# Beginning one layer's modulation vectors a stage earlier, with a result moved to another buffer

## The chip, the cores and the metric

The kernel runs on one core of a Trainium2 chip. The metric is the device time of one execution in microseconds (us), as the median of several runs. A core has five engines that work side by side, each through its own queue in order: TensorE (PE; its weight loads are PEld), VectorE (DVE), ScalarE (ACT), GpSimd (POOL) and SyncE (SP), which here issues nearly all the loads from memory. TensorE's clock has two levels, 1.2 and 2.4 GHz; the profile gives the granted clock as a share of the higher one.

## What the kernel computes

Two blocks are chained over 256 tokens of width 1024. Block 1 has 16 more tokens in front (272 in all) and two layers; block 2 has two layers, each with a vector of six modulation parts made from `c`. Cut to what matters here:

```python
# block 1, layer 0 ("ab"): attention and a convolution, then the output products
a = sliding_window_sink_attention(q, k, v, sinks) * silu(g_a)
c = silu(layer_norm(causal_depthwise_conv(u, conv_w, conv_b), ln_g, ln_b))
c = (c @ w_pw2) * silu(g_b)
y = concatenate([a, c], axis=-1) @ w_out
h = h + rms_norm(y, ab_post_norm)
# block 1, layer 1 ("sb")
y = (stick_breaking_attention(q, k, v) * silu(g)) @ w_out      # q, k, v, g = h' @ w_in
h = h + rms_norm(y, sb_post_norm)
# block 2, layer l: the modulation vectors, and what they are needed for
mod = (silu(c) @ ada_w[l] + ada_b[l]).reshape(6, D)            # ada_w[l]: 1024 x 6144
sh1, sc1, g1, sh2, sc2, g2 = mod
h = rmsnorm(x, norm_mix[l]) * (1 + sc1) + sh1                   # layer 0 ("ev"): mixer, then
x = x + g1 * mixer(h)
h = rmsnorm(x, norm_ffn[l]) * (1 + sc2) + sh2
x = x + g2 * peer(h, ...)                                       # a mixture of 16384 experts
```

`mod` depends on `c` alone, so it can be computed at any time before the "ev" layer uses it.

## The kernel before

**The main work.** Each product of a layer is cut into units of 512 KB of weights. `take` hands the next unit to the product, `load` fetches units some steps ahead into the ring `raw` (slots raw_70 and raw_71, two units each), and `prep` splits a unit into `hi` (ACT, L159) and `lo` (POOL, L261, partly DVE, L263), since most products are taken as three passes. The products of the "ab" layer use the weights as they come (kind "n"), so nothing is prepared for them, and DVE, ACT and POOL have little to do while its output products run. The order of all instructions is that in which the program is written; no scheduler moves them.

**Background work.** `after_unit` is called behind each unit. It emits the work that belongs to finished results (`pend`, `follow`, `hooks`) and then calls `tick(ns)`, which draws from two lanes of generators, `bgs` and `bg1`, as many steps as fit into `ns` (for bgs) and `ns1` (for bg1) nanoseconds of a nominal cost. What it draws is written into the engines' queues at that place.

**The modulation vectors** are such generators (`ada`, made by `ada_pool` into `ada0`). One step works on half a load, 128 x 512 numbers. In lane bgs a step is one DVE instruction (L677 or L679) at a nominal 660 ns, and after four loads the sum is transposed and reduced (L687, L688). In lane bg1 a step is a scaling on ACT and an addition on POOL (L675) at a nominal 1300 ns. The 40 loads (L654, 512 KB each, 32 for bgs and 8 for bg1) are issued on SP into the tile `scratch`, three buffers for bgs and two for bg1, each as soon as its buffer has been read; SP's queue waits there. The rest of the vectors (of layer 1, and the last two parts of layer 0) are made later, in the mixture.

**Where they run before.** `_build` puts ada0 into the lanes just ahead of `sb_layer`; its products tick 1400 ns a unit. What is left is drawn in the output products of "sb" and in the "ev" layer.

**The "ab" layer's end.** `linear_o(2, ...)` computes the output products in two halves (e = 0, 1) of four units. `need(0)`, at its start, waits out attention and convolution and drains the lanes; `need(2)` runs the layer norm and the product with `w_pw2` in between. `post_in` squares the results (ACT), adds the squares (DVE, L749, tile `absq`) and writes the scaled results to `y`: the first four by ACT, the last four by DVE (L757). `rest` then sums over partitions on PE, makes the reciprocal root (ACT, then DVE L485, L486, L488), and `add_post` scales, adds and writes the input `h` of the "sb" layer (DVE L772, POOL L778, ACT, DVE L527). `scratch` held the attention's scores and weights until then, and before the change it also holds `y`.

In the "sb" layer DVE scales the first products by the norm `sbr` (L1167), in the "ev" layer by the norm `r` (L1376, L1378); only then their PSUM banks are free for the next products (there are four banks with the tag "mm").

Of the kernel before, what the change touches and what calls it, by code (L numbers as in the profile page):

```python
# [43 lines left out]
KC = D // P  # L44
# [73 lines left out]
class _Kernel:  # L118
# [665 lines left out]
    def ab_layer(self, pool):  # L784
        nc, a, T = self.nc, self.a, T1
# [16 lines left out]
        ch = tl([P, KC, T], "cat")  # L802
        zh = tl([P, 4, T], "z")
        sc = self.scratch
# [245 lines left out]
        def layer_norm(rest):  # L1050

            sq = pool.tile([P, 4, T], F32, name="lnsq", tag="sq0")
            rl = pool.tile([P, T], F32, name="lnr")

            def total(x):
                ps = self.bank("aux")
                for c in range(4):
                    nc.tensor.matmul(ps[:, :T], self.ones, x[:, c, :], start=(c == 0), stop=(c == 3))
                return ps

            def mean():
                nc.gpsimd.tensor_add(cv[:, 2, :], cv[:, 2, :], part[:, 0, :])
                nc.gpsimd.tensor_add(cv[:, 3, :], cv[:, 3, :], part[:, 1, :])
                nc.vector.tensor_add(part[:, 2, :], part[:, 2, :], part[:, 3, :])
                nc.vector.tensor_add(cv[:, 3, :], cv[:, 3, :], part[:, 2, :])
                ps = total(cv)
                for c in range(4):
                    nc.vector.scalar_tensor_tensor(out=cv[:, c, :], in0=ps[:, :T], scalar=-1.0 / 512,
                                                   in1=cv[:, c, :], op0=ALU.mult, op1=ALU.add)
                    self.act(sq[:, c, :], cv[:, c, :], "Square")  # L1070

            def var():
                ps = total(sq)
                self.rsqrt(rl, ps[:, :T], 512, 1, pool, "")
                for c in range(4):
                    nc.vector.tensor_mul(cv[:, c, :], cv[:, c, :], rl)
                for c in range(4):
                    self.act(zh[:, c, :], cv[:, c, :], "Silu", scale=self.v["conv_ln_g"][:, c:c + 1],
                             bias=self.v["conv_ln_b"][:, c:c + 1])
                self.act(gb, gb, "Silu")  # L1080
            return [mean, var]
# [4 lines left out]
        def need(j):  # L1086
            if j == 0:
                while self.steps or self.follow or self.pend:
                    self.after_unit(800.0)
                self.drain()  # L1090
                self.hooks += layer_norm(None)
            if j == 2:
                self.flush()
                self.mark('ab_pw2')
                self.linear(2, (zh, None), T, c_out, kc=4, tags=("aux", "s"))
                self.flush()
# [2 lines left out]
        self.linear(11, (self.hn, None), T, consume, ns=2500, late=1)  # L1099
        self.pool_share = 0.5  # L1100
        self.mark('ab_out')
        y = sc[:, :KC * T].rearrange("p (c t) -> p c t", c=KC)
        sq = pool.tile([P, T], F32, name="absq", tag="vT")
        post = self.post_in(y, sq, self.v["ab_post_norm"], T, pool)
        self.linear_o(2, (ch, None), T, post, need=need)
        self.mark('ab_post')
        r2 = post.rest()
        nxt = self.scale(self.xT, self.v["sb_pre_norm"])
# [1073 lines left out]
def _build(ctx, tc, aps, const, out, stage=99, dbg=None):  # L2182
    ctx.enter_context(tc.manual_schedule())
    k = _Kernel(ctx, tc, aps, const)
    k.v_done = 0
    k.chain = stage == 99

    def phase(name):
        st = ExitStack()
        return st, st.enter_context(tc.tile_pool(name=name, bufs=1))  # L2190

    specs = []
    if stage in (1, 2, 99):
        specs += k.ab_specs() + k.sb_specs()
    if stage in (3, 4, 99):
        specs += k.ev_specs()
    if stage in (4, 99):
        specs += k.peer_specs(0)
    if stage in (5, 99):
        specs += k.od_specs()  # L2200
    if stage == 99:
        specs += k.peer_specs(1)
    k.plan(specs)
    k.mark('setup')
    pa = ExitStack()
    k.scratch = pa.enter_context(tc.tile_pool(name="ada", bufs=1)).tile([P, 7296], F32, name="scratch")
    ada0 = k.ada_pool(0, stage != 99)
    b1 = ExitStack()
    p1 = b1.enter_context(tc.tile_pool(name="block1", bufs=1))
    k.xT = p1.tile([P, KC, T1], F32, name="xT")  # L2210
    if stage in (1, 2, 99):
        st, pool = phase("ab")
        k.hn = pool.tile([P, KC, T1], F32, name="hn")
    k.setup()
    if stage in (1, 2, 99):
        k.ab_layer(pool)
        st.close()
        if stage > 1:
            with ExitStack() as st:
                pool = st.enter_context(tc.tile_pool(name="sb", bufs=1))  # L2220
                if stage == 99:
                    k.bgs += ada0[0]
                    k.bg1 += ada0[1]
                k.sb_layer(pool)
    if stage in (3, 4, 5):
        tc.nc.vector.tensor_copy(k.x2, k.xT[:, :, NM:])
    if stage != 1:
        b1.close()
    if stage in (3, 4, 99):
        k.mark('ev')  # L2230
        st, pool = phase("ev")
        if stage != 99:
            k.use_ps("aux")
            for g in ada0[0] + ada0[1]:
                for _ in g:
                    pass
        if not k.chain:
            nxt = k.enter(0, 0)
            for c in range(KC):
                nxt(c)  # L2240
        k.ev_layer(pool)
        st.close()
    pa.close()
    if stage in (4, 99):
        k.peer(0, k.ada_slots(1) if stage == 99 else None)
    if stage in (5, 99):
        k.mark('od')
        st, pool = phase("od")
        if stage == 5:
            k.use_ps("aux")  # L2250
            for g in sum(k.ada_pool(1), []):
                for _ in g:
                    pass
            for _ in k.angles(pool.tile([P, 770], F32, name="ang")):
                pass
        if not k.chain:
            nxt = k.enter(1, 0)
            for c in range(KC):
                nxt(c)
        k.od_layer(pool)  # L2260
        st.close()
    if stage == 99:
        k.peer(1, None, out)
    if dbg is not None:
        tc.nc.sync.dma_start(dbg[:, :, NM:], k.x2)
        tc.nc.sync.dma_start(dbg[:, :, :NM], k.x2[:, :, :NM])
# [21 lines left out]
```

## Time and profile before

| | |
|---|---|
| median of 3 runs | 2330.15 us (2322.14 to 2331.12) |
| profiled execution, its own time | 2316.25 us |
| its span, first to last instruction | 2314.5 us |
| busy: PE, PEld | 95%, 85% |
| busy: DVE, ACT, POOL | 76%, 56%, 75% |
| mean granted clock of TensorE | 0.984 |
| output products of "ab" | 127 to 175 us |
| "sb" layer | 180 to 367 us |
| "ev" layer | 374 to 462 us |

The profiled execution took 1.75 us more than its span, and 13.9 us less than the median of the runs. The modulation vectors of the lanes run from 193 us (first load) to 405 us (last reduction); the mixtures, which take most of the time, come after 462 us.

### The profile page before, as it was taken

What the parts mean: (1) busy time and instruction counts of PE and PEld (TensorE: products, weight loads), DVE (VectorE), ACT (ScalarE), POOL (GpSimd) and SP (SyncE); (2) the same over time, 40 slices, a digit from 0 to 9 for tenths busy, and PEclk for the clock granted to TensorE, in tenths of its full rate; (3) what the DMA queues carried; (4) which work ended last, traced back from release to release, by engine and by line L of the source; (5) the groups of instructions that cost most, each with busy time, mean ns of one, the idle gap of its engine ahead of it and who ended that gap; (6) DMA issues with size and microseconds to landing.
All of it is one profiled execution on the core that took longest, in us unless ns stands there. A gap on an engine that the chain in (4) does not pass through costs nothing. (4 is left out here: it accounts for less than half of the span.)

```text
span 2314.5 us, 42145 instructions
## 1 busy us (share of the span) xinstructions
PE 2194.9 (95%) x14789; PEld 1972.2 (85%) x14789; DVE 1763.1 (76%) x3502; ACT 1292.1 (56%) x2608; POOL 1735.9 (75%) x2070
## 2 busy tenths in 40 slices
PE   8997997899989999999999988998899999999997
PEld 6776987898989999888787877998889999888886
DVE  5927888578787999668989776786869998565555
ACT  2424575464436888544444645554458886545444
POOL 1106878788999988877576685579899888777776
PEclk9999998999999999999999999999999999999999
DMA  5326655378878778568888533687777876555554
GB/s 164 110 79 217 236 177 188 124 197 163 164 153 167 159 153 161 167 247 292 314 287 300 185 103 103 191 168 149 160 160 161 159 154 158 192 199 182 200 186 141
DMA packets 285582, 414.88 MB, mean 179 GB/s; under 512 B 16489, under 2 KB 217386, under 8 KB 285370
## 3 DMA queue, kind: packets, MB, share of 16 engines
q1 hardware_dynamic: 279722, 405.30, 63.7%
q10 hardware_dynamic: 5648, 6.89, 1.1%
q8 instruction: 116, 1.90, 0.4%
q14 instruction: 96, 0.79, 0.1%
HBM read 408.98 MB, written 3.15 MB: 178 GB/s over the span
## 5 line engine op out<-in xcount | busy, mean ns | idle before, releaser
L261 POOL TENSOR_TENSOR lo<-raw,hi 128x256 fp32r<-128x256 f32 x956 | 877.7, 946 | 378.2 <-ACT hi L159 354.7
L261 POOL TENSOR_TENSOR lo<-uT,hi 128x256 fp32r<-128x256 f32 x1022 | 780.8, 802 | 79.0 <-ACT hi L159 78.4
L159 ACT ACTIVATE hi<-raw 128x1024 fp32r<-128x1024 f32 x380 | 401.0, 1057 | 421.0 <-DMA raw<-in_peer_v 194.3
L2042 PE MATMUL mm<-h,hi 128*128 128x256 f32 x4096 | 531.8, 282 | 17.3 <-ACT hi L159 16.5
L2042 PEld LDWEIGHTS mm<-h,hi 128*128 128x128 f32 x4096 | 505.2, 190 | 20.9 <-ACT hi L159 18.9
L263 DVE TENSOR_TENSOR lo<-raw,hi 128x512 fp32r<-128x512 f32 (+1 forms) x290 | 226.0, 780 | 236.5 <-ACT hi L159 235.7
L231 DVE STREAM_TRANSPOSE uT<-raw 128x1024 f32<-128x1024 f32 x256 | 316.5, 1236 | 103.4 <-POOL lo L261 77.2
L159 ACT ACTIVATE hi<-uT 128x1024 fp32r<-128x1024 f32 x256 | 271.1, 1059 | 212.8 <-DVE uT L231 194.7
L2042 PE MATMUL mm<-h,lo 128*128 128x256 f32 x2048 | 312.1, 290 | 15.1 <-POOL lo L261 12.5
L2042 PEld LDWEIGHTS mm<-h,lo 128*128 128x128 f32 x2048 | 264.2, 189 | 27.9 <-POOL lo L261 27.8
L2093 PE MATMUL mm<-hi,whi 128*128 128x512 f32 x1024 | 277.1, 392 | 2.0 <-ACT hi L159 1.5
L2093 PE MATMUL mm<-hi,wlo 128*128 128x512 f32 x1024 | 274.8, 390 | 1.9 <-DVE wlo L494 1.8
L2093 PE MATMUL mm<-lo,whi 128*128 128x512 f32 x1024 | 275.3, 390 | 0.1
L2093 PEld LDWEIGHTS mm<-hi,whi 128*128 128x128 f32 x1024 | 191.1, 188 | 45.4 <-ACT hi L159 4.3
L2093 PEld LDWEIGHTS mm<-hi,wlo 128*128 128x128 f32 x1024 | 191.8, 188 | 43.8 <-DVE wlo L494 3.9
L2093 PEld LDWEIGHTS mm<-lo,whi 128*128 128x128 f32 x1024 | 191.3, 188 | 42.8 <-POOL lo L261 3.2
L406 PE MATMUL mm<-h,hi 128*128 128x258 f32 (+2 forms) x1344 | 206.9, 297 | 18.5 <-ACT h L159 8.5
L406 PEld LDWEIGHTS mm<-h,hi 128*128 128x128 f32 x1344 | 182.0, 197 | 24.4 <-ACT h L159 9.5
L1945 DVE TENSOR_TENSOR B<-sin,ij 128x512 f16<-128x512 bf16 x256 | 184.3, 757 | 0.0
L159 ACT ACTIVATE A<-B,cos 128x128 f32<-128x128 f16 x512 | 168.2, 404 | 0.1
L494 DVE TENSOR_TENSOR wlo<-slots,whi 128x256 fp32r<-128x256 f32 x192 | 158.0, 823 | 0.6
L406 PE MATMUL mm<-h,lo 128*128 128x258 f32 (+2 forms) x672 | 109.6, 297 | 4.0 <-POOL lo L261 3.6
(482 smaller groups left out, 2775.4 us busy)
## 6 DMA issues: line engine op xcount, KB each, us to landing
raw<-in_peer_u SPq DMA_DIRECT2D x512, 256.0 KB
raw<-in_peer_v SPq DMA_DIRECT2D x128, 1024.0 KB
slots<-in_ada_w SPq DMA_DIRECT2D x56, 512.0 KB
scratch<-in_ada_w SPq DMA_DIRECT2D x40, 512.0 KB
raw<-in_sb_w_in SPq DMA_DIRECT2D x32, 512.0 KB
raw<-in_peer_w_q SPq DMA_DIRECT2D x32, 512.0 KB
raw<-in_od_w_in SPq DMA_DIRECT2D x24, 512.0 KB
raw<-in_ab_w_in SPq DMA_DIRECT2D x22, 512.0 KB
```

The source lines that it names most:

```text
L159: self.nc.scalar.activation(out=out, in_=in_, func=getattr(ACTF, func), **kw)
L231: self.nc.vector.transpose(ut.rearrange("p b c e -> p c b e"), src)
L261: nc.gpsimd.tensor_sub(lo[:, sl], src[:, sl], hi[:, sl].bitcast(F32))
L263: nc.vector.tensor_sub(lo[:, n:], src[:, n:], hi[:, n:].bitcast(F32))
L406: nc.tensor.matmul(ps[mm][:, :T], w[:, o:o + P], x[:, j * 4 + kk, :T], start=(j == 0 and n_of[mm] == 1), stop=(j == nu - 1 and n_of[mm] == ...
L494: nc.vector.tensor_sub(lo, src, hi.bitcast(F32))
L1945: nc.vector.tensor_tensor(out=B.rearrange("p j n i -> p j (n i)"), in0=iota4, in1=ij[:, g].rearrange("p n i -> p (n i)").unsqueeze(1).to_b ...
L2042: nc.tensor.matmul(ps[:, :T], w[:, c * P:(c + 1) * P], x[:, c, :], start=(pas == 0 and c == 0), stop=(pas == 2 and c == KC - 1))
L2093: nc.tensor.matmul(outs[t][d], w[:, t * P:(t + 1) * P], v[:, 512 * d:512 * d + 512], start=(i == 0 and pas == 0), stop=(i == P - 1 and pas ...
```

## The change

The generators are put into the lanes in `need(0)` of the "ab" layer, behind the drain, and no longer ahead of `sb_layer`. Their small products take PSUM banks with the tag "aux" from there on. `y` of the "ab" layer is written to `hn`, the tile that held the layer's normalised input, because `scratch` now receives the loads. The output products tick 2500 ns a unit in place of the default 1600 (before, the lanes were empty there).

```diff
@@ need(j) in ab_layer
                     self.after_unit(800.0)
                 self.drain()
                 self.hooks += layer_norm(None)
+                self.use_ps("aux")
+                for lane, gens in zip((self.bgs, self.bg1), self.ada0):
+                    lane += gens
             if j == 2:
                 self.flush()
                 self.mark('ab_pw2')
@@ ab_layer
-        y = sc[:, :KC * T].rearrange("p (c t) -> p c t", c=KC)
+        y = self.hn
         sq = pool.tile([P, T], F32, name="absq", tag="vT")
         post = self.post_in(y, sq, self.v["ab_post_norm"], T, pool)
-        self.linear_o(2, (ch, None), T, post, need=need)
+        self.linear_o(2, (ch, None), T, post, need=need, ns=2500)
@@ _build
     ada0 = k.ada_pool(0, stage != 99)
+    k.ada0 = ada0 if stage == 99 else ((), ())
...
-                if stage == 99:
-                    k.bgs += ada0[0]
-                    k.bg1 += ada0[1]
                 k.sb_layer(pool)
```

Lines behind L1091 move by three.

DVE at the end of the "ab" layer, before: the last of the three additions of squares of the first half, then the low parts of the first two units of "sb", the last additions, the four scalings into y and the reciprocal root.

```order
L749 TENSOR_TENSOR absq<-absq,psq_1064 128x272
L263 TENSOR_TENSOR lo_1092<-raw_70,hi_1091 128x512
L263 TENSOR_TENSOR lo_1106<-raw_70,hi_1105 128x512
L749 TENSOR_TENSOR absq<-absq,psq_1114 128x272
L749 TENSOR_TENSOR absq<-absq,psq_1119 128x272
L757 TENSOR_SCALAR scratch<-mm_1068,vec 128x272
```

The same place now, from the last of the three additions (another number, the same instruction) to the first scaling into y:

```order
L749 TENSOR_TENSOR absq<-absq,psq_1089 128x272
L677 TENSOR_SCALAR scratch<-scratch,cact 128x512
L679 SCALAR_TENSOR_TENSOR scratch<-scratch,cact 128x512 x7
L687 STREAM_TRANSPOSE scratch<-scratch 128x512
L688 TENSOR_REDUCE scratch<-scratch 128x16
...
L679 SCALAR_TENSOR_TENSOR scratch<-scratch,cact 128x512
L263 TENSOR_TENSOR lo_1141<-raw_70,hi_1140 128x512
L679 SCALAR_TENSOR_TENSOR scratch<-scratch,cact 128x512 x4
L263 TENSOR_TENSOR lo_1164<-raw_70,hi_1163 128x512
L749 TENSOR_TENSOR absq<-absq,psq_1172 128x272
...
L757 TENSOR_SCALAR hn<-mm_1100,vec 128x272
```

Between those two, 17 steps of the modulation vectors (L677, L679) and two transposes with their reductions now stand: 8 steps and a pair, 2 steps, one low part, 4 steps, the other low part, the two additions, 2 steps and a pair, 1 step, and then the scalings. Further on, four more steps stand between the sum of squares of "sb" (L550) and its reciprocal root, and two between that and the first scaling by it (L1167).

DVE in the "ev" layer, before, from the sum of squares to the first scaling by r:

```order
L550 TENSOR_TENSOR sq_3364<-sq_3364 128x256
L679 SCALAR_TENSOR_TENSOR scratch<-scratch,cact 128x512
L687 STREAM_TRANSPOSE scratch<-scratch 128x512
L688 TENSOR_REDUCE scratch<-scratch 128x16
L677 TENSOR_SCALAR scratch<-scratch,cact 128x512
L679 SCALAR_TENSOR_TENSOR scratch<-scratch,cact 128x512
L485 SCALAR_TENSOR_TENSOR nw_3478<-r 128x256
...
L679 SCALAR_TENSOR_TENSOR scratch<-scratch,cact 128x512 x2
L1376 COPY b_3519<-mm_3366 128x1
```

And now:

```order
L550 TENSOR_TENSOR sq_3385<-sq_3385 128x256
L485 SCALAR_TENSOR_TENSOR nw_3493<-r 128x256
L486 SCALAR_TENSOR_TENSOR nw_3493<-aux_3491,nw_3493 128x256
L488 SCALAR_TENSOR_TENSOR r<-nw_3493,r 128x256
L1379 COPY b_3531<-mm_3387 128x1
```

No step is left in "ev", nor in the output products of "sb": the last sum of the lanes (L698) now stands between the second and the third of the four gate products of "sb".

SP's queue, now, from the third unit of the output products to the second of "sb" (ab_w_out and sb_w_in are units of weights, ada_w the loads of the modulation vectors):

```order
L654 DMA scratch<-in_ada_w 128x2x512 x3
L310 DMA raw_71<-in_ab_w_out 128x2x512 x2
L654 DMA scratch<-in_ada_w 128x2x512
L310 DMA raw_70<-in_ab_w_out 128x2x512
L654 DMA scratch<-in_ada_w 128x2x512 x2
...
L654 DMA scratch<-in_ada_w 128x2x512 x3
L294 DMA raw_70<-in_sb_w_in 128x4x256
L654 DMA scratch<-in_ada_w 128x2x512
L294 DMA raw_70<-in_sb_w_in 128x4x256
```

Before, the weights stood there alone. From the third load of ab_w_out to the load that the last of the 17 steps reads, 21 loads now stand in this queue, 8 of weights and 13 of ada_w; of the 40 loads of the lanes, 19 stand ahead of the fourth unit of "sb" in place of none.

## Rows read from the trace of the kernel before

**Rows 1.** Windows: length, busy us per engine, granted clock, DMA share, GB/s.

```profile
190.00:212.00 22.00, 17.86 (x126) 15.82 (x124) 16.20 (x28) 11.14 (x14) 18.34 (x22) 1.00 0.96 319
212.00:240.00 28.00, 24.94 (x155) 22.45 (x155) 21.10 (x36) 15.23 (x25) 22.93 (x26) 0.88 0.71 241
300.00:341.00 41.00, 38.56 (x305) 34.18 (x304) 36.08 (x69) 27.41 (x53) 31.16 (x38) 1.00 0.50 170
```

**Rows 2.** Waits of PE, 180 to 250 us: total us, times, longest.

```profile
PE mm L406 <- DVE sbq L1167: 2.5, 2, 1.5
PE s L1244 <- DVE z L1250: 1.6, 1, 1.6
PE s L1261 <- DVE z L1250: 1.5, 1, 1.5
```

**Rows 3.** Waits of PE, 250 to 340 us.

```profile
PE s L1261 <- DVE z L1266: 1.7, 1, 1.7
PE s L1244 <- DVE z L1250: 0.7, 1, 0.7
```

**Rows 4.** Waits of PE, 340 to 372 us.

```profile
PE mm L457 <- POOL lo L261: 1.9, 3, 1.0
PE aux L476 <- DVE sbsq L749: 0.6, 1, 0.6
```

**Rows 5.** Waits of PE, 372 to 440 us.

```profile
PE mm L406 <- DVE sb L1378: 5.0, 1, 5.0
```

**Rows 6.** Timeline of DVE, end of "ab": start, us, instruction, [idle before <- releaser].

```profile
148.76 0.83 DVE L1084 TENSOR_TENSOR cat<-aux,gb 128x272 f32<-128x272 f32 x2 [4.92 <-PE aux L406]
...
160.58 0.44 DVE L749 TENSOR_TENSOR absq<-absq,psq 128x272 f32<-128x272 f32 x1 [0.47 <-ACT psq L159]
168.77 0.69 DVE L263 TENSOR_TENSOR lo<-raw,hi 128x512 fp32r<-128x512 f32 x1 [7.75 <-ACT hi L159]
...
174.61 1.71 DVE L757 TENSOR_SCALAR scratch<-mm,vec 128x272 f32<-128x272 f32 x4
177.50 0.44 DVE L485 SCALAR_TENSOR_TENSOR nw<-postr 128x272 f32<-128x272 f32 x1 [1.17 <-ACT postr L159]
```

**Rows 7.** Tile scratch, whole span: count, ns min/median/max, first and last start.

```profile
L679 DVE SCALAR_TENSOR_TENSOR scratch<-scratch,cact x56: 733/1102/1670, 206.1 to 401.5; 128x512 f32<-128x512 f32 x56
...
L675 POOL TENSOR_TENSOR scratch<-scratch x14: 1267/1490/1749, 216.2 to 302.3; 128x512 f32<-128x512 f32 x14
L687 DVE STREAM_TRANSPOSE scratch<-scratch x10: 696/708/714, 215.6 to 404.1; 128x512 f32<-128x512 f32 x10
```

**Rows 8.** Timeline of DVE, start of "sb".

```profile
199.32 0.85 DVE L485 SCALAR_TENSOR_TENSOR nw<-sbr 128x272 f32<-128x272 f32 x1 [2.94 <-ACT sbr L159]
```

**Rows 9.** Timeline of ACT, "sb".

```profile
220.55 0.72 ACT L159 ACTIVATE scratch<-scratch,cact 128x512 f32<-128x512 f32 x1 [3.72 <-DMA scratch<-in_ada_w]
```

**Rows 10.** Timeline of DVE, "ev".

```profile
393.02 0.94 DVE L485 SCALAR_TENSOR_TENSOR nw<-r 128x256 f32<-128x256 f32 x1
...
394.80 2.34 DVE L679 SCALAR_TENSOR_TENSOR scratch<-scratch,cact 128x512 f32<-128x512 f32 x2
397.06 0.14 DVE L1376 COPY b<-mm 128x1 f32<-128x1 f32 x1
```

**Rows 11.** Timeline of ACT, "ev".

```profile
389.87 0.51 ACT L159 ACTIVATE r<-r,eps 128x256 f32<-128x256 f32 x1
```

**Rows 12.** Timeline of PE, "ev".

```profile
397.68 2.06 PE L406 MATMUL mm<-h,hi 128*128 128x258 f32 x8 [5.02 <-DVE sb L1378]
...
403.40 1.21 PE L406 MATMUL mm<-h,hi 128*128 128x258 f32 x8
```

**Rows 13.** Timeline of POOL, output products of "sb".

```profile
340.18 3.02 POOL L261 TENSOR_TENSOR lo<-raw,hi 128x256 fp32r<-128x256 f32 x4 [1.50 <-ACT hi L159]
...
348.42 23.77 POOL L261 TENSOR_TENSOR lo<-raw,hi 128x256 fp32r<-128x256 f32 x28 [1.74 <-ACT hi L159]
```

**Rows 14.** Timeline of SP's queue: the six later units of ab_w_out.

```profile
132.50 28.00 SPq L310 DMA_DIRECT2D raw<-in_ab_w_out  x6
```

## The prediction, made before the changed kernel was run

> **What bounds the kernel now.** I read the windows first, then PE's waits stretch by stretch, then the timelines of the engines it waits for. The windows show PE as the engine that sets the pace: in the "sb" layer it is busy 24.9 of 28 us and 38.6 of 41 us, with DVE and POOL close behind [rows 1]. So the steps of the modulation vectors cost time only where PE waits for an engine on which one of them stood ahead. The waits name such places. At the start of "sb" PE waits 2.5 us for the first scaling by sbr and 3.1 us for additions to scores [rows 2]; in its second half 2.4 us for DVE again [rows 3]; in its output products 1.9 us for POOL and 0.6 us for DVE [rows 4]; in "ev" 5.0 us in one piece, for the first scaling by r [rows 5]. At the end of "ab", on the other hand, DVE is idle most of the time: 4.92 us ahead of one instruction and 7.75 us ahead of another [rows 6]. The change takes steps from the first kind of place to the second. But the end of "ab" has a tail that nothing covers, from the last squares over the reciprocal root to the first input of "sb", and DVE is on it.
>
> **What it costs: the tail of "ab".** Behind the third addition of squares, which ends at 161.02 us [rows 6], DVE now has 17 steps, two transposes with reductions, two low parts, two additions and the four scalings before the reciprocal root L485. A step took 0.733 us at least and 1.102 in the median [rows 7]; a transpose 0.71, its reduction counted the same; a low part 0.69; an addition 0.44; the scalings 1.71 together [rows 6, 7]. With 0.73 a step the sum is 12.4 + 2.8 + 1.4 + 0.9 + 1.7 = 19.2 us and L485 starts at 180.2; with 1.10 it is 25.5 us and 186.5. It started at 177.50 [rows 6]. So the tail comes 2.7 to 9.0 us later, if no load is late. I take 0.9 a step, since POOL is less busy here than in "sb", where the medians come from: 17 steps are 15.3 us, the sum is 22.1 us, L485 starts at 183.1, and PE gets its first input of "sb" **5.6 us** later. That is late for everything behind it: the constants and units of "sb" wait for buffers that this tail frees.
>
> **The first products of "sb".** Four steps now stand ahead of the reciprocal root of "sb"; it waited 2.94 us for ACT [rows 8], which hides most of 2.9 to 4.4 us; six tiny instructions that also stood there are gone. Two more stand between the root and L1167, for which PE waits already [rows 2]: 1.5 to 2.2 us, I take **1.9**. Sum of the costs: **7.5 us** (4.2 to 12.7, with 1.5 for the root when steps are slow).
>
> **What costs nothing, and its cover.** The first two steps behind the layer norm lie in DVE's 4.92 us [rows 6]; without that cover they would cost their 1.5 us. y in hn is written by the same instructions with the same shapes, into a tile whose last reader is long done. The small products are the same in another bank. Of the loads, three stand ahead of the third unit of the output products; it was issued at 132.5 us [rows 14], and PE reads it only behind the product with w_pw2, half of which DVE takes at 148.76 [rows 6], so it has 16 us. The others are in rival (3). The five steps that POOL now gets at the end of "ab" fall where it does two low parts, and behind ACT's scalings, which ACT does in its waits for PE.
>
> **What it gives back.** (a) Start of "sb". At 220.55 us ACT's queue stood 3.72 us before a scaling whose load had not landed [rows 9], with copies behind it that DVE waited for; PE then waited 3.1 us [rows 2], and the granted clock of 212 to 240 us is 0.88, so about 28 x 0.12 = 3.4 us went to the lower level of 1.2 GHz [rows 1]. Together 6.5 us. But lane bg1 still has four of its eight loads to come there, and the refill of the ring that crowds them (319 GB/s at a DMA share of 0.96 from 190 us on [rows 1]) stays. Bounds 0 and 6.5; between them I take half, **3.2**. (b) Second half of "sb": the last steps stood there, and none does behind the second gate product: 2.4 us of waits [rows 3], of which I take **2.0** (0 to 2.4). (c) Output products: POOL took 23.77 / 28 = 0.85 us a piece beside DVE's steps and 3.02 / 4 = 0.755 ahead of them [rows 13]; 28 x 0.094 = 2.6 us, of which PE waited 1.9 [rows 4]: **1.9** (0 to 2.6). With the 0.6 us for the sum of squares [rows 4], which one step held up: **0.6**. (d) "ev". ACT has r ready at 390.38 us [rows 11], but DVE starts L485 at 393.02, and two more steps of 2.34 us stand ahead of L1376 [rows 10]: 2.64 + 2.34 = 5.0 us, just PE's wait [rows 5]. Behind that wait a group of eight matmuls takes 2.06 us, and 1.21 us once the clock is back [rows 12]; three groups of that kind make 2.4 us more. Together **7.4** (0 to 7.4; the lower end if something else is next in line). Sum of the gains: **15.1 us** (0 to 19.3).
>
> The Trainium skill's page "TensorE: Matmul & The Clock Gate" (Part 1: The HAM clock gate) says that a stall puts the array at half rate, which it leaves only after sustained work. That agrees with [rows 12]; by it the wait of PE at the end of "ab", which gets longer, would be followed by slow matmuls as well, but they are paced by DVE there, so the sum above stays as it is.
>
> **The sum.** 2316.25 + 7.5 - 15.1 = 2308.7 us for the profiled execution, a change of -7.6 us. The median of the runs lies 13.9 us above the profiled time, so I forecast 2330.15 - 7.6, about **2322.5 us**: 0.3% less. A measurement of this kernel can tell about 0.5% (11.7 us) from no change, so this would count as the same.
>
> **Rivals.**
> (1) The gains come whole and the steps run as if alone: +4.2 - 19.3 = -15 us, 2315 us. For it: [rows 9] and [rows 5] are single pieces that may vanish whole. Against it: 21 of the 40 loads of the lanes still come in "sb", at the same pace.
> (2) DVE and POOL exclude each other in the tail. The five additions of POOL at 1.27 us at least [rows 7] and four low parts of 0.755 [rows 13] make 9.4 us; if DVE stands still for all of it, the tail is 19.2 + 9.4 = 28.6 us, L485 starts at 189.6, 12.1 us late in place of 5.6, and the change is -1 us: 2329 us. For it: the spread of L679 from 733 to 1670 ns [rows 7]. Against it: medians of 1102 where POOL is busy nearly all the time. The Trainium skill's page "SBUF — State Buffer" (Who interferes with whom) says that a DVE instruction with two inputs in SBUF and a POOL instruction that reads SBUF block each other; by that rule this rival would be the forecast, and the trace agrees in kind, not in size.
> (3) The other side: the loads don't keep up. 21 loads of 0.524 MB, 11.0 MB, must land after 132.5 us, when the third unit was issued [rows 14], before the last of the 17 steps can run. At 319 GB/s [rows 1] that takes 34.5 us, which is hidden; at 241 GB/s 45.7 us, hidden still. It decides below about 197 GB/s: then the last load lands at 188.3 us, and with a step and the scalings (2.4 us) L485 is about 13.2 us late, which with the 1.9 above eats the gains. At 170 GB/s, the rate of 300 to 341 us [rows 1], the load lands at 197.2, L485 is 22.1 us late, and the change is 22.1 + 1.9 - 15.1 = +9 us: 2339 us. For it: SP's queue stops at each load until its buffer is read, so loads don't overlap freely, and DVE's low parts wait for units behind those loads. Against it: 170 GB/s was what was asked for there, at a DMA share of 0.50.
> (4) The gain in "ev" isn't there, since another wait takes its place (weights, POOL's low parts): -0.2 us, 2330 us. Against it: PE had its inputs, and only banks were missing [rows 5].
>
> **How the numbers follow.** Chances: forecast 0.52 (its own range 2316 to 2329), rival (1) 0.20, (2) 0.10, (3) 0.09, (4) 0.09. The range from 2310 to 2337 us takes in (1), (2) and (4) and the runs' own spread, and leaves out the worse part of (3) and a still better (1). Faster by over 0.5%: (1) with most of its weight and a little of the forecast's lower edge, 0.24. Slower by over 0.5%: the far part of (3), 0.08. Within 0.5%: 0.68.
>
> **What the profile would show.** Right: L485 of the output norm of "ab" 3 to 9 us later, with steps and not a wait for a load ahead of it on DVE; PE idle that much longer before the first product of "sb"; no wait of PE for L1381 (L1378 before) in "ev" and no slow groups there; POOL at about 0.77 us a piece in the output products of "sb". The 3.72 us stop of ACT is the least certain. Wrong: a wait for `scratch<-in_ada_w` or for `raw<-in_sb_w_in` on DVE or ACT in the tail (rival 3), or a new wait of PE in "ev" where the old one was (rival 4).

## The result, and the profile after

The changed kernel took 2333.24 us in the median of 20 runs (2322.75 to 2344.35), the kernel before 2320.42 beside it (20 runs, 2310.09 to 2331.12): a ratio of 1.0062 (95% interval 1.0048 to 1.0076). It is slower by 0.6%, some 13 us, where a gain of 7.6 us was forecast. The profiled execution took 2340.03 us; what follows the stretches below, the mixtures above all, took 11.7 us more in it than in the execution shown before, while the runs of the kernel before lie up to 21 us apart, so only the stretches ahead of the mixtures are compared.

Five starts mark these stretches: the third addition of squares of "ab" (DVE, [rows 6]), the reciprocal root L485 of its output norm, PE's first product of "sb", its first output product of "sb", its first product of "ev", and its wait for `ycat` late in "ev". Times in us, from the timelines:

| | before | after | difference | forecast |
|---|---|---|---|---|
| tail of "ab": third addition to L485 | 16.92 | 30.17 | +13.25 | +5.6 |
| "sb": first product to first output product | 160.68 | 163.24 | +2.56 | -3.3 |
| output products, to the first of "ev" | 32.90 | 34.22 | +1.32 | -2.5 |
| "ev", to the wait for ycat | 65.09 | 59.54 | -5.55 | -7.4 |
| all | 278.54 | 290.11 | +11.57 | -7.6 |

(From L485 to the first product of "sb" it is 2.94 us in both.) Each column is one profile. A second one of a kernel that has "sb" and "ev" as before (`y_only`, below) gave 161.68, 34.11 and 64.51 us for the last three stretches, 1.6 us more in all, so a difference of 1 us in one row says little; the tail was 16.88 us there.

The windows of the tail: first two rows of the kernel before, then all of the changed one, with three that answer to [rows 1].

```profile
149.00:163.00 14.00, 14.00 (x63) 11.61 (x62) 2.80 (x7) 3.11 (x8) 0.00 (x0) 1.00 0.44 150
163.00:176.00 13.00, 13.00 (x58) 10.48 (x56) 4.36 (x8) 3.59 (x6) 4.03 (x4) 1.00 0.38 123
```

```profile
132.50:149.00 16.50, 12.82 (x49) 10.01 (x48) 6.42 (x19) 10.07 (x15) 0.00 (x0) 0.90 0.27 95
149.00:163.00 14.00, 14.00 (x63) 11.61 (x62) 10.16 (x18) 4.67 (x11) 0.88 (x1) 1.00 0.85 297
163.00:176.00 13.00, 12.29 (x54) 9.86 (x52) 9.47 (x10) 0.27 (x1) 4.04 (x3) 1.00 0.88 275
176.00:186.00 10.00, 0.00 (x0) 0.00 (x0) 8.24 (x8) 4.48 (x8) 7.96 (x6) 0.66 0.78 264
190.00:212.00 22.00, 15.02 (x85) 13.49 (x85) 19.70 (x30) 11.61 (x19) 13.98 (x15) 0.84 0.38 123
212.00:240.00 28.00, 22.34 (x153) 20.74 (x152) 25.33 (x34) 10.72 (x14) 25.92 (x27) 0.88 0.76 255
300.00:341.00 41.00, 41.00 (x306) 36.70 (x305) 32.84 (x61) 25.15 (x45) 25.57 (x31) 1.00 0.49 159
```

The DMA engines go from a share of 0.44 to 0.85 and stay near it to 186 us, and PE does nothing at all from 176 to 186 us. What it waits for, on DVE's timeline (answers to [rows 6]):

```profile
161.09 0.44 DVE L749 TENSOR_TENSOR absq<-absq,psq 128x272 f32<-128x272 f32 x1 [0.47 <-ACT psq L159]
...
161.97 8.14 DVE L679 SCALAR_TENSOR_TENSOR scratch<-scratch,cact 128x512 f32<-128x512 f32 x7
...
177.55 0.69 DVE L263 TENSOR_TENSOR lo<-raw,hi 128x512 fp32r<-128x512 f32 x1 [4.80 <-ACT hi L159]
178.16 5.15 DVE L679 SCALAR_TENSOR_TENSOR scratch<-scratch,cact 128x512 f32<-128x512 f32 x4
183.23 1.21 DVE L263 TENSOR_TENSOR lo<-raw,hi 128x512 fp32r<-128x512 f32 x1
...
189.62 1.72 DVE L757 TENSOR_SCALAR hn<-mm,vec 128x272 f32<-128x272 f32 x4
191.26 0.43 DVE L485 SCALAR_TENSOR_TENSOR nw<-postr 128x272 f32<-128x272 f32 x1
```

A step takes 8.14 / 7 = 1.16 and 5.15 / 4 = 1.29 us, and the first low part waits 4.80 us for ACT, which waits for weights. SP's queue and ACT, before:

```profile
163.81 7.70 SPq L294 DMA_DIRECT2D raw<-in_sb_w_in  x3
...
167.69 1.06 ACT L159 ACTIVATE hi<-raw 128x1024 fp32r<-128x1024 f32 x1 [6.76 <-DMA raw<-in_sb_w_in]
```

and after:

```profile
166.10 3.34 SPq L654 DMA_DIRECT2D scratch<-in_ada_w  x3
169.53 0.42 SPq L294 DMA_DIRECT2D raw<-in_sb_w_in  x1
...
176.46 1.06 ACT L159 ACTIVATE hi<-raw 128x1024 fp32r<-128x1024 f32 x1 [13.20 <-DMA raw<-in_sb_w_in]
...
180.23 1.24 ACT L159 ACTIVATE psq<-mm 128x272 f32<-128x272 f32 x4
```

The first weights of "sb" are issued 5.7 us later, behind three loads of the vectors, and are there 6.9 us after that in place of 3.9. ACT's last squares stand behind them. What SP's queue waited for from 132 to 186 us:

```profile
SPq L654 <- DVE scratch L679: 21.0, 8, 7.3
...
SPq L310 <- PE aux L406: 10.2, 1, 10.2
```

The loads of the vectors stand 21.0 us for buffers that DVE's steps have yet to read. The wait of 10.2 us, for a buffer of weights that the product with w_pw2 reads, was there before (10.7).

PE's waits in the changed kernel, in "sb" (answers to [rows 2]), the output products ([rows 4]) and "ev" ([rows 5]); the last row is the wait for vz in the kernel before:

```profile
PE mm L406 <- DVE sbq L1170: 4.9, 1, 4.9
...
PE s L1264 <- DVE z L1253: 2.4, 1, 2.4
PE aux L554 <- DVE sq L550: 1.9, 1, 1.9
PE s L1247 <- DVE z L1253: 1.4, 1, 1.4
...
PE aux L476 <- DVE sbsq L749: 3.5, 1, 3.5
...
PE s L1362 <- DVE vz L1354: 6.2, 1, 6.2
...
PE mm L406 <- DVE sb L1381: 0.2, 1, 0.2
```

```profile
PE s L1359 <- DVE vz L1351: 4.3, 1, 4.3
```

The wait of 5.0 us in "ev" is gone, as forecast, and so are the waits for POOL in the output products. But the wait for sbq grew from 2.5 to 4.9 us, the wait for the sum of squares from 0.6 to 3.5, and the wait for vz from 4.3 to 6.2.

### The profile page after: what moved, and what is told of

It reads as the page before. It is cut to its first block, busy times and chain, and to the rows that moved or that the text cites. A ratio compares the mean times of both kernels' runs of the same rounds, so it can differ in the third digit from the quotient of the medians.

```text
span 2338.3 us, 42151 instructions
## 1 busy us (share of the span) xinstructions
PE 2205.2 (94%) x14789; PEld 1981.5 (85%) x14789; DVE 1769.1 (76%) x3502; ACT 1291.7 (55%) x2608; POOL 1724.4 (74%) x2070
## 5 line engine op out<-in xcount | busy, mean ns | idle before, releaser
L261 POOL TENSOR_TENSOR lo<-raw,hi 128x256 fp32r<-128x256 f32 x956 | 868.2, 937 | 344.7 <-ACT hi L159 322.4
L406 PEld LDWEIGHTS mm<-h,hi 128*128 128x128 f32 x1344 | 181.7, 197 | 21.0 <-ACT h L159 10.3
```

Of the source, the lines that this page charges most:

```text
L261: nc.gpsimd.tensor_sub(lo[:, sl], src[:, sl], hi[:, sl].bitcast(F32))
L406: nc.tensor.matmul(ps[mm][:, :T], w[:, o:o + P], x[:, j * 4 + kk, :T], start=(j == 0 and n_of[mm] == 1), stop=(j == nu - 1 and n_of[mm] == ...
```

## The experiments

The theories after this comparison: (1) the loads come late, the weights behind them; (2) DVE's steps themselves fill the tail; and as a part of (2), GpSimd's additions hold those steps up (the prediction's rival 2). Numbers below are by the stretches of the table, each from one profile; a single time is one execution.

**Loads out, steps short, both.** `noload` (lines in the function `load` of `ada`), `thin` (in its steps) and `noload_thin` with both:

```diff
             p, k2 = divmod(n, 4)
+            if l == 0 and (1 <= n <= 3 if pool else p0 == 0 and 3 <= n <= 12):
+                return
...
-                    nc.vector.scalar_tensor_tensor(out=acc, in0=x, scalar=s, in1=acc, op0=ALU.mult, op1=ALU.add)
+                    c = 16 if l == 0 and p0 == 0 and n < 13 else 512
+                    nc.vector.scalar_tensor_tensor(out=acc[:, :c], in0=x[:, :c], scalar=s, in1=acc[:, :c],
+                                                   op0=ALU.mult, op1=ALU.add)
```

> The changed kernel without 13 of the 40 loads of the modulation vectors: the loads 4 to 13 of lane bgs and 2 to 4 of lane bg1 are left out, and their steps work on what lies in the buffers, so the vectors are not the reference's. All instructions of DVE, ACT and POOL stay. In the changed kernel the reciprocal root of the output norm of "ab" (L485) starts at 191.26 us, 13.8 us later than before (177.50), and PE's first product of "sb" at 194.20. Theory 1, loads: the low parts and ACT's hi of the first units of "sb" wait for weights whose loads stand behind those of the vectors in SP's queue, and the squares and additions stand behind these in the queues. Then hi of the first unit no longer waits 13.2 us for raw<-in_sb_w_in, L485 starts near 182 to 184 us and the first product of "sb" near 185 to 187. Theory 2, DVE's own time: 17 steps at 1.16 to 1.29 us beside POOL, and the tail is as late as in the changed kernel, L485 at 189 to 192.

> The changed kernel with all its loads, but the multiply-add steps of the first 13 loads of lane bgs (L679) work on 16 of 512 columns, so the vectors are not the reference's. Theory 1, loads: the wait of ACT's hi for raw<-in_sb_w_in stays (13.2 us in the changed kernel) and L485 of the output norm of "ab" starts at 184 us or later (191.26 in the changed kernel, 177.50 before). Theory 2, DVE's own time: the tail comes back to within 3 us of before, L485 at 177.5 to 180.5 and the first product of "sb" at 180.5 to 183.5.

> Both edits at once: 13 loads of the modulation vectors left out, and the multiply-add steps of the first 13 loads of lane bgs on 16 of 512 columns. Both theories: nothing is left in the tail but the transposes with their reductions (2.8 us), so L485 starts at 177.5 to 181 us. Together with the two single runs it gives the shares: if loads and steps add up, the delays of the two single runs sum to the delay that this run takes away; if one hides the other, they don't.

The tail took 24.34 us without the loads, 26.52 with short steps, 18.49 with both (30.17 changed, 16.92 before); L485 came at 184.66, 189.21 and 179.05; the single times were 2325.28, 2332.28 and 2314.32 us. Neither theory is enough: each single edit leaves a tail over 7 us too long. Nor do the two simply add up: they take away 5.83 and 3.65 us alone and 11.68 together, so about 2.2 us of the steps hide behind the wait for loads. Without the loads (ACT, then DVE):

```profile
167.38 1.06 ACT L159 ACTIVATE hi<-raw 128x1024 fp32r<-128x1024 f32 x1 [4.88 <-DMA raw<-in_sb_w_in]
```

```profile
161.19 8.60 DVE L681 SCALAR_TENSOR_TENSOR scratch<-scratch,cact 128x512 f32<-128x512 f32 x7
...
172.60 1.22 DVE L263 TENSOR_TENSOR lo<-raw,hi 128x512 fp32r<-128x512 f32 x1
```

the weights are in time again, and the low part follows DVE's own steps without a wait. But seven steps still take 8.60 us; and in `thin` seven steps of 16 columns took 4.96 us, where one alone took 0.23. So a third thing slows them.

**GpSimd's additions short**, with and without the 13 loads (`thinpool`, `noload_thinpool`):

```diff
-                        nc.gpsimd.tensor_add(acc, acc, x)
+                        c = 16 if l == 0 and n < 4 else 512
+                        nc.gpsimd.tensor_add(acc[:, :c], acc[:, :c], x[:, :c])
```

> The run without the 13 loads, and besides GpSimd's additions to the first four loads of lane bg1 (L675) work on 16 of 512 columns; the vectors are not the reference's. It asks why a step took 1.2 us in the tail and 0.73 elsewhere. From the third addition of squares to L485 it was 24.3 us without the loads, 18.5 with the steps thin as well, 16.9 before. If GpSimd's additions hold DVE's steps up: seven steps take 5.1 to 5.5 us in place of 8.6, and the stretch 19.5 to 21.5 us. If the steps are slow for another reason: 23.5 us or more.

> The changed kernel with all loads and all of DVE's steps, but GpSimd's additions to the first four loads of lane bg1 on 16 of 512 columns; the vectors are not the reference's. In the changed kernel the stretch from the third addition of squares to L485 was 30.2 us: 16.5 to the first low part, which waits for weights, and 13.7 behind it. If loads set the first part and GpSimd's additions lengthen only the second: 15.5 to 16.5 and 11 to 12.5 us, 27 to 29 us in all. If the additions were what is late (the second rival of the prediction): 21 to 24 us.

Without loads (DVE of `noload_thinpool`, then of `thinpool`):

```profile
170.04 5.48 DVE L682 SCALAR_TENSOR_TENSOR scratch<-scratch,cact 128x512 f32<-128x512 f32 x7
```

```profile
175.36 0.69 DVE L263 TENSOR_TENSOR lo<-raw,hi 128x512 fp32r<-128x512 f32 x1 [4.06 <-ACT hi L159]
...
187.15 0.43 DVE L485 SCALAR_TENSOR_TENSOR nw<-postr 128x272 f32<-128x272 f32 x1
```

Seven steps take 5.48 us: 0.78 each. With all of DVE's steps in place the tail is:

| tail, us | GpSimd's additions short | whole |
|---|---|---|
| 13 loads left out | 20.56 | 24.34 |
| all loads | 26.46 | 30.17 |

These two do add up: over the 16.92 us before, DVE's steps and transposes cost 3.64 us, GpSimd's additions 3.78 or 3.71, the loads 5.90 or 5.83. Each cell is one profile; where a tail was profiled twice with nothing changed in it, the two differed by 0.3 and 0.7 us (the changed kernel 30.17, `thin_sbq` 29.84; `quiet3` 25.77, `quiet3b` 25.08). In `thinpool` the third addition also came 1.1 us later behind the product with w_pw2 than in the other three; counted from that product, the additions cost 3.78 or 2.63 and the loads 6.98 or 5.83. So each share is good to about 1 us. That late start also fits the stretch up to the first low part (14.67 us) and the whole (26.46), which are a little shorter than was expected of `thinpool`; the second rival's 21 to 24 us is ruled out. The single times were 2318.96 and 2319.71 us, against 2321.14 for one run of the kernel before beside them.

**Loads on another queue** (`gq`), in `load`:

```diff
-            nc.sync.dma_start(raws[n % nbuf], w[k2 * 256:(k2 + 1) * 256, c0:c0 + 512]
+            q = nc.gpsimd if l == 0 and (n <= 3 if pool else p0 == 0 and n <= 12) else nc.sync
+            q.dma_start(raws[n % nbuf], w[k2 * 256:(k2 + 1) * 256, c0:c0 + 512]
```

> The changed kernel with the loads of the modulation vectors that fall into the "ab" layer (the first 13 of lane bgs, the first 4 of lane bg1) issued by GpSimd in place of SyncE; nothing is left out. It asks why the weights of "sb" come late: because they stand behind those loads in SP's queue, which stops at each until its buffer is read, or because both share the DMA engines. From PE's product with w_pw2 to L485 of the output norm it was 34.0 us before, 47.3 in the changed kernel, 41.4 without the loads. Queue order: the first load of sb_w_in is issued at 164 us after a start of w_pw2's product at 144 (before 163.8; changed 169.5), lands in about 4 us, and the stretch takes 41 to 43 us. Shared engines: it is issued at 164 but lands 6 to 10 us later, and the stretch takes 44 to 47 us.

SP's queue, ACT and DVE of this run:

```profile
165.12 7.70 SPq L294 DMA_DIRECT2D raw<-in_sb_w_in  x3
...
170.80 1.06 ACT L159 ACTIVATE hi<-raw 128x1024 fp32r<-128x1024 f32 x1 [6.74 <-DMA raw<-in_sb_w_in]
178.72 0.72 ACT L159 ACTIVATE scratch<-scratch,cact 128x512 f32<-128x512 f32 x1 [6.86 <-DMA scratch<-in_ada_w]
...
180.49 4.22 DVE L680 SCALAR_TENSOR_TENSOR scratch<-scratch,cact 128x512 f32<-128x512 f32 x2 [2.49 <-DMA scratch<-in_ada_w]
```

The weights are issued in time and land 5.7 us later, but now the vectors' loads are what DVE and ACT stand before. From the product with w_pw2 to L485 it is 46.3 us, in the range given to the shared engines, though the weights came a little sooner than was put there (6 to 10 us). The tail is 29.18 us, the ratio to before 1.0033 (1.0003 to 1.0064). So in this run the order of the queue decided which load is late, and hardly how long the tail is. (GpSimd's queue holds these loads now, eight of 0.72 us each in the tail; what a queue of their own would do isn't shown.)

**The six steps at the root of "sb"** made short (`thin_sbq`), and these together with `noload_thin` (`gains`): the condition for `c = 16` is `(12, 1) <= (n, k) <= (15, 0)`, and `(n, k) <= (15, 0)`.

> The changed kernel with the six multiply-add steps that stand around the reciprocal root of "sb" (four between the sum of squares L550 and the root, two between that and the first scaling L1170) on 16 of 512 columns, so the vectors are not the reference's. The tail of "ab" is as in the changed kernel: L485 at 190 to 193 us. From PE's first product of "sb" to its first output product of "sb" it was 160.7 us before (180.45 to 341.13) and 163.2 in the changed kernel (194.20 to 357.44). Theory: these six steps make PE wait 4.9 us in place of 2.5 and drop the granted clock behind that wait, 5 to 6 us in all; then this stretch takes 157 to 159 us, PE's wait for L1170 is at most 2.5 us and the clock stays above 0.9 behind it. Rival: the stretch is paced by the loads and by POOL, and the steps cost only the 1.9 us forecast; then it takes 161 to 163 us.

> The changed kernel without the 13 loads and with all multiply-add steps of lane bgs up to the first scaling by sbr on 16 of 512 columns (both costs of the change taken away, its gains left in); the vectors are not the reference's. If the gains are what was forecast, 15.1 us, PE's first product with ycat in "ev" after its wait for ACT comes about 13 us earlier than before (439.12 us, so at 425 to 427). If the gains are only what the other runs show, 3 us from the cheap tail's run and 4 to 6 from the six steps, it comes at 431 to 434 us, and the one time is near 2308 to 2312 us, within the spread of the runs.

"sb" took 160.01 us with `thin_sbq`, 3.2 less than in the changed kernel and between what the two sides expected; PE still waited 3.2 us for the scaling (two waits), and the granted clock still fell to 0.57 from 222 to 230 us, so the six steps are not all of what delays it. (`y_only`, with "sb" as before, had 161.68.) With `gains` 160.40, and ycat came at 434.73 us (just past the upper end of 431 to 434, far from 425 to 427). Their single times were 2328.57 and 2309.51 us. From the third addition to ycat `gains` takes 274.08 us, 4.5 less than before: 6.0 less behind the tail and 1.6 more in it.

`thin_sbq` showed one thing more: its output products took 29.75 us. DVE's last two additions of squares with GpSimd's row beside them, there and in the changed kernel:

```profile
382.15 1.84 DVE L751 TENSOR_TENSOR sbsq<-sbsq,psq 128x256 f32<-128x256 f32 x2 [8.29 <-ACT psq L159]
...
365.83 20.79 POOL L261 TENSOR_TENSOR lo<-raw,hi 128x256 fp32r<-128x256 f32 x28 [1.74 <-ACT hi L159]
```

```profile
379.80 4.94 DVE L749 TENSOR_TENSOR sbsq<-sbsq,psq 128x256 f32<-128x256 f32 x2 [8.27 <-ACT psq L159]
...
369.45 14.48 POOL L261 TENSOR_TENSOR lo<-raw,hi 128x256 fp32r<-128x256 f32 x20
```

GpSimd works without a stop beside both, yet the additions take 1.84 us in one and 4.94 in the other. In `gains` they took 4.91 and the output products 34.19. In `thinpool`, where they took 1.84, the three stretches are 160.27, 29.75 and 58.06 us, 10.6 less than before behind the tail. So there was more to gain than the 6.0 of `gains` shows, and these additions hold about 4.4 us of it.

**The gain of "ev" without the tail** (`ev1800`: before, with `ns = 1800` in place of `ns = 1400` in `sb_layer`), and **y alone** (`y_only`: before, with `y = self.hn`).

> The kernel before with one number changed: the products of "sb" tick 1800 ns a unit in place of 1400, so that no step of the modulation vectors is left in "ev"; the "ab" layer is untouched and nothing is left out. It tries the gain in "ev" alone, without the tail. From PE's first product of "ev" to its product behind the wait for ycat it was 65.1 us before and 58.1 in three of the runs without steps there. Theory: this stretch takes 58 to 59 us, and "sb" gives back 0 to 3 us, so the time is 4 to 7 us below that of the kernel before (0.2 to 0.3%). Rival: DVE and POOL are full in "sb", and the denser steps cost there what "ev" gains: within 2 us of before.

> The kernel before with one part of the change alone: y of the "ab" layer is written to hn in place of scratch; nothing is left out. All theories: no change, within 3 us of the kernel before, L485 at 177 to 178 us; its profile is also a second look at the kernel before.

`ev1800` was slower, which neither side expected: ratio 1.0045 (1.0026 to 1.0064). "ev" took 59.61 us (-5.5), but "sb" 167.38 (+6.7) and the output products 39.01 (+6.1). Its waits in "sb" and the output products:

```profile
PE s L1261 <- DVE z L1250: 3.2, 1, 3.2
PE mm L406 <- DVE sbq L1167: 3.1, 2, 2.8
...
PE mm L457 <- DVE sbo_lo L1143: 3.1, 2, 2.6
PE s L457 <- DVE z L1266: 2.4, 1, 2.4
```

`y_only` changed nothing: 0.9998 (0.9977 to 1.0019), the tail 16.88 us.

**Fewer steps in "ab"**: `quiet3` and again `quiet3b` (`quiet=3` in the call of `linear_o`), `p5` (as `quiet3`, with no tick in the first product of "sb"), `p7` (as `p5`, with `ns=1600`), `p4` (`ns=1320, quiet=3`).

> The changed kernel with no step of the lanes drawn behind the last three units of the output products of "ab"; no part of the computation is left out. The steps that stood in the tail come in "sb". Theory 1 and theory 2 both expect the tail to come back: L485 at 178 to 183 us (191.26 in the changed kernel), since steps and loads both go. If the gain in "ev" of 5 us (no wait of PE for the first scaling by r) stays, since the lanes still end ahead of "ev", the time is 4 to 9 us below that of the kernel before, 16 to 21 us below the changed one. If what is taken from the tail comes back as waits in "sb", the time is within 4 us of the kernel before.

> The run with the last three units quiet, once more, for a second profile: its first profiled execution was the slowest of its 12. If that profile is typical, the stretch from the third addition of squares to the wait for ycat is 288 to 290 us again (before 278.5); if its late stages were an accident of that execution, it is 279 to 284.

> The changed kernel with fewer steps in "ab": its output products tick 1600 ns in place of 2500, none is drawn behind the last three units, and none in the first product of "sb"; nothing is left out. 9 steps and transposes stand in "ab" in place of 28 to 32, 3 between the root of "sb" and L1170 in place of 6 around the root, none in "ev". By the cost of loads and steps in the tail, L485 comes 2 to 5 us later than before (177.5 us); "ev" takes 58 to 59.5 us from its first product to the wait for ycat (65.1 before). If "sb" and its output products take no longer than in the changed kernel, the time is 1 to 5 us below that of the kernel before; if the steps that now come in "sb" cost there what they did with the 1800 ns tick (6.7 us in "sb" and 6 in its output products), it is 3 to 8 us above.

> As the run with 1600 ns, but with a tick of 1320 ns in "ab" and the first product of "sb" ticking as in the changed kernel: 7 steps in "ab", 7 around the root of "sb", 2 in the output products of "sb", none in "ev". L485 2 to 4 us later than before; the steps at the root cost about 3 us as in the changed kernel; within 4 us of the kernel before either way.

> The changed kernel with the tick of 2500 ns in "ab", none drawn behind its last three units, and none in the first product of "sb": 16 steps in "ab", 2 around the root of "sb", none in its output products nor in "ev". The tail is as in the run with the last three units quiet (44 us from the product with w_pw2 to L485, 34.0 before), and the stretch from the first product of "sb" to its output products is 2.5 to 3.5 us shorter than there (163.3), since the steps at the root are gone; if it isn't, the steps there only change place.

| | tail | "sb" | output products | "ev" | ratio to before |
|---|---|---|---|---|---|
| quiet3 | 25.77 | 163.29 | 38.71 | 58.09 | 0.9998 (0.9982 to 1.0015) |
| quiet3b | 25.08 | 162.25 | 33.00 | 59.58 | one run, 2326.32 us |
| p7 | 18.67 | 160.66 | 37.93 | 59.52 | 0.9993 (0.9968 to 1.0017) |
| p4 | 20.09 | 163.76 | 36.94 | 58.07 | 1.0002 (0.9976 to 1.0028) |
| p5 | 25.26 | 167.58 | 39.86 | 58.05 | one run, 2333.92 us |

All of them get 5.5 to 7 us in "ev" and pay for it elsewhere; of the three timed more than once none beats the kernel before. The interval of `p7` (7 us below to 4 above) can't tell its two sides apart. In `p5` the steps at the root only changed place, and "sb" got longer. In `quiet3` both theories expected L485 at 178 to 183 us; it came at 186.26. Ten of the 17 steps were gone from the tail, but three loads of the vectors still stood ahead of the first weights, and ACT's row is

```profile
176.65 1.06 ACT L159 ACTIVATE hi<-raw 128x1024 fp32r<-128x1024 f32 x1 [14.60 <-DMA raw<-in_sb_w_in]
```

(in `p7` that wait is 7.69 us, and the tail 18.67). This agrees with `thin`: with loads ahead of the first weights the tail stays long, whatever the steps. The profiles of `quiet3` and `quiet3b`, the same kernel, show 10.3 and 4.3 us more than before up to ycat, the timed runs no difference; the first was the slowest of its 12 runs, and 5.7 us between the two profiles are the output products'. Most of these are one addition of squares:

```profile
377.92 5.41 DVE L749 TENSOR_TENSOR sbsq<-sbsq,psq 128x256 f32<-128x256 f32 x1 [8.63 <-ACT psq L159]
```

```profile
384.55 0.65 DVE L749 TENSOR_TENSOR sbsq<-sbsq,psq 128x256 f32<-128x256 f32 x1 [8.58 <-ACT psq L159]
```

The rest stays open.

## Why the prediction was wrong

The change went the other way: 13 us slower, not 7.6 faster. That 2333.24 us lies between 2310 and 2337 is luck. The forecast stood on a median of three runs, 2330.15, and 20 runs gave 2320.42; with the measured ratio the base of the prediction would give 2330.15 x 1.0062 = 2344.6 us.

**The tail (5.6 us forecast, 13.25 measured) is the step that failed first**, at "if no load is late". DVE's share was in its bounds: with GpSimd's additions it is 3.64 + 3.78 = 7.4 us, inside the 2.7 to 9.0 given. But 5.9 us of waiting for loads came on top. Rival (3) had the cause and the wrong test: it asked when the last of 21 loads would land, at 170 to 319 GB/s from 132.5 us on. What counted was when the first weights of "sb" came: they were issued late, because SP stood for buffers that DVE's steps had to free, and landed late; and in-order queues put the remaining steps behind the low parts that wait for these weights, so that most of the steps' time comes behind the loads' and not beside it. The mean rate from 132.5 to 186 us is (16.5 x 95 + 14 x 297 + 13 x 275 + 10 x 264) / 53.5 = 223 GB/s, above the 197 below which rival (3) was to decide; that its 13.2 us is close to the measured 13.25 is a coincidence. The sign that the prediction had named for it came, ACT's wait of 13.20 us for raw<-in_sb_w_in, but 6.76 us of that wait stood there before the change.

**Rival (2)** had its mechanism right, and its size too large: GpSimd's additions in the tail were busy for about 8.5 us and cost 3.7, not 9.4 with the low parts.

**The first products of "sb"** (1.9 us forecast) cost 3.2 us by `thin_sbq`, where profiles of one stretch differ by about 1 us. The four steps ahead of the root took 5.19 us where 2.9 to 4.4 were put, more than the 2.94 us that hide them [rows 8]. And the longer wait lets the clock fall, which no term had:

```profile
216.20:224.20 8.00, 4.44 (x20) 4.15 (x21) 7.65 (x13) 0.00 (x0) 8.00 (x10) 0.57 0.85 290
```

```profile
219.67 2.60 PE L406 MATMUL mm<-h,hi 128*128 128x272 f32 x8 [4.87 <-DVE sbq L1170]
```

The granted clock is 0.57 here, and a group of eight matmuls takes 2.60 us, 1.16 to 1.27 for its like at full clock. That fall isn't the change's alone: in `y_only`, where PE waits 2.9 us there in two pieces, it is the same behind them, while it was 1.00 in the profile before (2.5 us):

```profile
199.00:207.00 8.00, 6.92 (x33) 6.70 (x33) 7.00 (x11) 1.37 (x2) 6.09 (x9) 0.57 0.97 319
```

**The gains (15.1 us forecast) were the second failure.** (The upper bounds add up to 19.5 us, not 19.3.) Taken with the 1.9 above, 13.2 us were to come back behind the tail; 1.7 did, or 3.3 against `y_only`. So even a tail of 5.6 us would have ended 3.9 us slower than before. (a) The start of "sb", 3.2: nothing came. ACT waits less for the vectors' loads, 2.4 us in all in "sb" in place of 9.9, but a longer stop of another kind stands there now, for a buffer that DVE has yet to transpose:

```profile
225.39 0.72 ACT L159 ACTIVATE scratch<-scratch,cact 128x512 f32<-128x512 f32 x1 [10.44 <-DVE scratch L687]
```

PE's waits for the scores' additions are 2.4 + 1.4 where they were 1.6 + 1.5 [rows 2]. Whether ACT's stop ever caused them isn't shown. (b) The second half, 2.0: came; PE's waits from 260 us to the end of "sb" are 0.2 us, and the lag behind the kernel before falls from 19.5 us at 246 us to 16.3 at the first output product. (c) The output products, 1.9 + 0.6: POOL runs at 14.48 / 20 = 0.72 us a piece and PE no longer waits for it, as forecast; but DVE's two additions took 4.94 us beside it, and the sum of squares came 3.5 us late. Where they took 1.84 (`thin_sbq`, and 1.84 and 1.86 in the runs with short additions of GpSimd) the stretch was 29.75 to 29.78 us, 3.2 less than before: the gain exists, and the slow additions take it back. What makes them slow isn't shown: GpSimd's row is the same beside the quick ones, and one kernel (`quiet3`, `quiet3b`) had both. (d) "ev", 7.4: 5.0 of waiting gone, but the wait for vz grew from 4.3 to 6.2 us: 5.55 in all, 7.0 in the runs where it was 5.2.

The Trainium skill, "SBUF — State Buffer" (Who interferes with whom), says that a DVE instruction with two inputs in SBUF contends with a GpSimd instruction that reads SBUF. The trace agrees in the tail (1.16 to 1.29 us a step beside GpSimd's additions and low parts, 0.78 without the additions), and in (c) where the additions are slow; that a long run of GpSimd instructions can hold an addition for 5.4 us, and need not, is the measurement's own.

**What was right:** y in hn costs nothing; the first loads lie hidden behind w_pw2's product; no new wait stands where the one of 5.0 us was. Rival (4) holds only for the 1.9 us by which the wait for vz grew.

## What to carry to other kernels

An engine that looks idle at the end of a layer may stand there because a chain waits on it: price moved work by the chain behind it, with every load that shares the way. When loads are moved ahead of weights, ask when the first weights behind them arrive and what is queued behind those, not when the last load lands. And where two engines are full in a stage, work taken out of a later wait and put there can come back as another wait: `ev1800` gained 5.5 us in "ev" and lost 12.8 ahead of it.

## What was not expected of the hardware

Two additions of 128x256 on DVE took 1.1 to 1.9 us in nine of the 17 profiles, 4.91 to 4.94 in six, 3.59 and 5.84 in the other two, of the same shape and each time beside GpSimd's row of low parts. In a slow case the addition ends just behind that row (`quiet3`: 383.33 us, the row 383.05), as if it had been held until GpSimd stopped; what decides between quick and slow stays open. Steps of 16 columns, 0.23 us alone, took 4.96 us for seven beside three GpSimd additions. So the time of a DVE instruction here can be set by its neighbour and not by its size.
